# An MLP's two products by seven block products instead of eight, with squared activations kept in DRAM

## The chip, the cores and the metric

The kernel runs on one core of a Trainium2 chip. The metric is the device time of one execution in microseconds. A core has five engines that run side by side and each take their instructions in a fixed order: TensorE (PE in the profile; PEld is its loading of weights), VectorE (DVE), ScalarE (ACT), GpSimd (POOL) and SyncE (SP), which here issues the transfers between DRAM and the on-chip memory SBUF. TensorE writes its sums into eight banks of a second memory, PSUM.

## The reference, cut to what matters

A trunk of two layers over 1024 tokens of width 1024. Each layer has a token mixer, a cross-attention into 256 memory tokens and an MLP with 4096 hidden features (d_ff); each of the three starts with an RMSNorm and ends with a residual sum. All is float32.

```python
def rmsnorm(x, g):
    y = x * lax.rsqrt(jnp.mean(x * x, axis=-1, keepdims=True) + EPS)
    return y * g

def sq_relu_mlp(h, w_in, w_out):          # (1024, 1024) @ (1024, 4096), then @ (4096, 1024)
    return jnp.square(jax.nn.relu(h @ w_in)) @ w_out

for i in range(DEPTH):                    # DEPTH = 2
    ...
    h = h + sq_relu_mlp(rmsnorm(h, norm_mlp[i]), mlp_w_in[i], mlp_w_out[i])
return rmsnorm(h, norm_final)
```

## The kernel before

Everything lies feature by token: a tile is 128 features by 512 tokens, so the residual stream x is eight tiles for each of two chunks c of 512 tokens. To keep float32's precision with TensorE's faster format (fp32r), every operand is split into a high part h, rounded by ScalarE, and a low part l, the exact rest, a subtraction (`split_l`, L89) on GpSimd or VectorE. `mm3` (L101) makes a product of three matmuls: h·h, h·l, l·h. One matmul has a 128x128 block of weights and 512 columns of activations.

`load_w` (L91) loads 128x512 weights through SP's queue and splits them: ScalarE rounds (L97), GpSimd subtracts (L89).

The norm in front of a product is spread around it: `ready` (L201) takes a finished tile of x, multiplies it with the norm's gain (`gain_split`, L188 to L192) and splits it, before 1/rms is known; the sum of squares is gathered on the way (`Norm.add`, L123), and 1/rms is multiplied into the product's result.

`mlp` (L844) goes over d_ff in 8 parts of four tiles. `win(f)` (L848) makes one tile of d_ff for both chunks: 8 x 3 matmuls each, then VectorE multiplies with 1/rms (L854) and makes relu and square in one operation (L855), ScalarE rounds (L858), GpSimd subtracts (L859). For each part, `ounit` (L870) multiplies it with its rows of w_out, eight tiles of outputs for each chunk with 4 x 3 matmuls each, and VectorE adds the result to x (L233). The squared activations g never leave SBUF. An MLP has 2 x 1536 = 3072 matmuls.

Tiles come from pools with a number of slots by tag, used in turn (2 KB per partition each); a tile can be written when the last reader of its slot is done:

```python
SLOTS = dict(x=16, a=32, g=24, o=8, p=6, f=4, raw=3, w=8, pt=4, tmp=5)
PSLOTS = dict(s=3, pt=2, acc=3)
```

Which instruction follows which on an engine is set by a scheduler when the program is built, within what data and slots allow. At run time the order is fixed, and an engine that waits holds up all that stands behind it.

## Time and profile before

| | |
|---|---|
| three runs | 2743.97, 2744.0, 2748.67 us; median 2744.0 |
| span of the profiled execution | 2743.0 us |
| TensorE busy | 2662.9 us, 97% |
| VectorE, ScalarE, GpSimd busy | 1373.9, 970.3, 1029.2 us |
| a stretch in the first MLP, 640 to 1300 us | TensorE busy 660.0 of 660 us |
| a stretch in the second MLP, 2030 to 2680 us | TensorE busy 650.0 of 650 us |

An engine is busy while it works on an instruction. Matmuls are pipelined, so the busy time of one is longer than the distance between two; the distance tells how fast TensorE goes. "PEclk" is the granted share of TensorE's full clock: 1.00 is 2.4 GHz, 0.50 is 1.2 GHz.

### The profile page before, as it was taken

What the parts mean: (1) busy time and instruction counts of PE and PEld (TensorE: products, weight loads), DVE (VectorE), ACT (ScalarE), POOL (GpSimd) and SP (SyncE); (2) the same over time, 40 slices, a digit from 0 to 9 for tenths busy, and PEclk for the clock granted to TensorE, in tenths of its full rate; (3) what the DMA queues carried; (4) which work ended last, traced back from release to release, by engine and by line L of the source; (5) the groups of instructions that cost most, each with busy time, mean ns of one, the idle gap of its engine ahead of it and who ended that gap; (6) DMA issues with size and microseconds to landing.
All of it is one profiled execution on the core that took longest, in us unless ns stands there. A gap on an engine that the chain in (4) does not pass through costs nothing.

```text
span 2743.0 us, 34762 instructions
## 1 busy us (share of the span) xinstructions
PE 2662.9 (97%) x13446; PEld 2239.1 (82%) x13446; DVE 1373.9 (50%) x2504; ACT 970.3 (35%) x1956; POOL 1029.2 (38%) x788
## 2 busy tenths in 40 slices
PE   8899999999999999999999999999999999999997
PEld 6788889787888888888888888877878888888886
DVE  6777776874222222223475766687762222222227
ACT  7677676552111111112343333345531111111112
POOL 3543235544333333343423232246253333333332
PEclk9999999999999999999999999999999999999998
DMA  3000003111111111111111010122021111111111
GB/s 118 28 23 23 27 21 97 31 43 46 54 50 50 43 46 58 47 50 35 32 32 39 24 39 24 39 70 62 24 62 46 54 43 46 54 46 52 38 50 62
DMA packets 70164, 125.48 MB, mean 46 GB/s; under 512 B 7792, under 2 KB 12656, under 8 KB 70000
## 3 DMA queue, kind: packets, MB, share of 16 engines
q1 hardware_dynamic: 69856, 123.15, 15.1%
q8 instruction: 105, 1.72, 0.3%
q14 instruction: 59, 0.48, 0.1%
q10 hardware_dynamic: 144, 0.13, 0.0%
HBM read 119.05 MB, written 4.19 MB: 45 GB/s over the span
## 4 chain that ended last, share of the span: by engine, by line
PE 82%; DVE 12%; ACT 2%; issue 2%; POOL 1%; DMA 0%; SPq 0%; DVEq 0%; ACTq 0%; POOLq 0%
PE ps_acc L104 16%; PE ps_acc L103 16%; PE ps_acc L102 16%; PE ps_s L104 9%; PE ps_s L102 9%; PE ps_s L103 9%; PE ps_s L370 4%; DVE f L434 2%; PE ps_pt L392 2%; DVE a L192 2%; DVE p L439 1%; DVE x L233 1%; DVE tmp L131 1%; DVE tmp L181 1%; PE ps_s L775 1%
## 5 line engine op out<-in xcount | busy, mean ns | idle before, releaser
L89 POOL TENSOR_TENSOR w<-raw,w 128x512 fp32r<-128x512 f32 (+1 forms) x293 | 385.4, 1317 | 586.8 <-ACT w L97 567.0
L233 DVE TENSOR_TENSOR x<-ps_acc,x 128x512 f32<-128x512 f32 x408 | 278.1, 686 | 331.8 <-PE ps_acc L104 330.2
L97 ACT CAST w<-raw 128x512 fp32r<-128x512 f32 (+1 forms) x293 | 178.8, 611 | 438.4 <-PE ps_s L103 209.2
L102 PE MATMUL ps_acc<-a,w 128*128 128x512 f32 (+1 forms) x776 | 300.9, 388 | 10.1 <-DVE tmp L349 5.2
L104 PE MATMUL ps_acc<-a,w 128*128 128x512 f32 (+1 forms) x776 | 301.0, 388 | 1.0 <-POOL w L89 1.0
L103 PE MATMUL ps_acc<-a,w 128*128 128x512 f32 (+1 forms) x776 | 299.3, 386 | 1.6 <-DVE a L192 1.5
L89 POOL TENSOR_TENSOR g<-tmp,g 128x512 fp32r<-128x512 f32 x120 | 158.2, 1320 | 295.8 <-ACT g L184 237.3
L89 POOL TENSOR_TENSOR g<-pt,g 128x512 fp32r<-128x512 f32 x96 | 124.3, 1294 | 278.9 <-ACT g L858 278.9
L233 DVE TENSOR_TENSOR x<-ps_s,x 128x512 f32<-128x512 f32 x120 | 82.9, 691 | 228.1 <-PE ps_s L104 228.1
L858 ACT CAST g<-pt 128x512 fp32r<-128x512 f32 x96 | 59.5, 620 | 349.9 <-DVE pt L855 349.9
L102 PEld LDWEIGHTS ps_acc<-a,w 128*128 128x128 f32 x776 | 147.5, 190 | 39.7 <-DVE tmp L349 5.8
L854 DVE TENSOR_TENSOR pt<-ps_acc,tmp 128x512 f32<-128x512 f32 x64 | 44.1, 691 | 259.8 <-PE ps_acc L104 251.0
L103 PEld LDWEIGHTS ps_acc<-a,w 128*128 128x128 f32 x776 | 147.4, 190 | 31.9 <-DVE a L192 5.0
L104 PEld LDWEIGHTS ps_acc<-a,w 128*128 128x128 f32 x776 | 147.4, 190 | 30.1 <-POOL w L89 1.4
L89 POOL TENSOR_TENSOR p<-raw,p 128x512 fp32r<-128x512 f32 x73 | 97.2, 1331 | 175.6 <-ACT p L97 161.7
L854 DVE TENSOR_TENSOR pt<-ps_s,tmp 128x512 f32<-128x512 f32 x64 | 44.2, 691 | 236.9 <-PE ps_s L104 233.7
L104 PE MATMUL ps_s<-g,w 128*128 128x512 f32 (+1 forms) x378 | 148.2, 392 | 0.0
L102 PE MATMUL ps_s<-g,w 128*128 128x512 f32 (+1 forms) x378 | 148.0, 392 | 0.0
L103 PE MATMUL ps_s<-g,w 128*128 128x512 f32 (+1 forms) x378 | 148.0, 391 | 0.0
L102 PE MATMUL ps_acc<-g,f 128*128 128x512 f32 (+1 forms) x377 | 146.2, 388 | 0.0
L103 PE MATMUL ps_acc<-g,f 128*128 128x512 f32 (+1 forms) x377 | 146.2, 388 | 0.0
L104 PE MATMUL ps_acc<-g,f 128*128 128x512 f32 (+1 forms) x377 | 145.9, 388 | 0.0
(242 smaller groups left out, 7001.6 us busy)
## 6 DMA issues: line engine op xcount, KB each, us to landing
raw<-in_w_in SPq DMA_DIRECT2D x128, 256.0 KB, 2.6
raw<-in_w_out SPq DMA_DIRECT2D x128, 256.0 KB, 2.6
x<-in_xT SPq DMA_DIRECT2D x16, 256.0 KB, 5.1
raw<-in_w_mo SPq DMA_DIRECT2D x16, 256.0 KB, 2.7
raw<-in_w_xk SPq DMA_DIRECT2D x16, 256.0 KB, 2.7
raw<-in_w_xv SPq DMA_DIRECT2D x16, 256.0 KB, 2.7
raw<-in_w_xq SPq DMA_DIRECT2D x16, 256.0 KB, 2.6
raw<-in_w_xo SPq DMA_DIRECT2D x16, 256.0 KB, 2.6
```

What stands on the lines that cost most here:

```text
L89: eng.tensor_tensor(out=l, in0=full, in1=h.bitcast(F32), op=ALU.subtract)
L97: nc.scalar.copy(out=h, in_=raw)
L102: nc.tensor.matmul(out=ps, lhsT=wh, rhs=xh, start=start, stop=False, skip_group_check=True)
L103: nc.tensor.matmul(out=ps, lhsT=wh, rhs=xl, start=False, stop=False, skip_group_check=True)
L104: nc.tensor.matmul(out=ps, lhsT=wl, rhs=xh, start=False, stop=stop, skip_group_check=True)
L192: nc.vector.scalar_tensor_tensor(out=l, in0=xt, scalar=g, in1=h.bitcast(F32), op0=ALU.mult, op1=ALU.subtract)
L233: nc.vector.tensor_tensor(out=x[c][f], in0=ps, in1=x[c][f], op=ALU.add)
L370: nc.tensor.matmul(out=ps[:, :n], lhsT=lh, rhs=rh, start=(i == 0), stop=(i == len(passes) - 1), skip_group_check=True)
L392: nc.tensor.transpose(out=tp[:, o0:o0 + P], in_=col(probs[qi][kb // 4], kb % 4), identity=ident)
L434: nc.vector.tensor_tensor_scan(out=rev, data0=rev, data1=pt[j][:, :n], op0=ALU.mult, op1=ALU.bypass, initial=1.0 if j == len(pieces) - 1 e ...
L854: nc.vector.tensor_tensor(out=t, in0=ps, in1=r[c], op=ALU.mult)
L858: nc.scalar.copy(out=h, in_=t)
```

## The change

Both products of the MLP are cut into 2x2 blocks and made by Strassen's scheme in the form with 15 sums: seven block products instead of eight. For C = A·B with A a block of weights (transposed) and B activations, the chunks of tokens are B's two column halves. The weights' sums are S1 = A21 + A22, S2 = S1 - A11, S3 = A11 - A21, S4 = A12 - S2; those of B are T1 to T4. Products go into three banks: A11·B11 and then A12·B21 on top of it, S2·T2, S3·T3 and A22·T4 in the second, S1·T1 and S4·B22 in the third; VectorE and ScalarE read a bank between two products (`e1` to `e7`).

The first four of the 32 tiles of d_ff are left as they were (their squares go to DRAM and come back at the end); the other 28 are taken in 14 pairs. `ready` now waits for 1/rms and makes normalised tiles; `quad` makes T1 to T4 of them. `win` makes one pair: four loads of weights, `weight_sums` (four sums on VectorE, seven splits by ScalarE and GpSimd), seven products of 12 matmuls, relu and square, and the sums T1 to T4 for the second product, four operations; seven tiles are stored to DRAM. After all pairs, `fetch` loads and splits a pair's seven tiles, and `wout` adds the last up to four pairs to two tiles of outputs for both chunks; over 17 steps each of four such output pairs takes all 14.

```diff
     def ready(c, f, gcol):
+        if gcol in (G_MLP, G_MLP + 8):
+            norm[c].add(x[c][f], nc.vector if f % 2 else nc.gpsimd)
+            if f == FT - 1:
+                rms[c], norm[c] = norm[c].finish(), Norm(D)
+                for k in range(FT):
+                    t = T("p")
+                    normed(t, c, k, gcol)
+                    act[c].append(split(t, "a", nc.vector if k % 2 else nc.gpsimd))
+            return
...
+    SEVEN = (("A11", "B11", 0), ("S2", "T2", 1), ("A12", "B21", 0), ("S3", "T3", 1), ("S1", "T1", 2), ("A22", "T4", 1),
+             ("S4", "B22", 2))
...
+    def weight_sums(load, n):
+
+        w, pe, ve = n * P, nc.gpsimd, nc.vector
+        a11, a12, a21, a22 = (load(q, ("raw", "f", "raw", "f")[q]) for q in range(4))
+        s1, s2 = T("tmp")[:, :w], T("tmp")[:, :w]
+        r = {"A11": split(a11, "w", pe)}
+        tt(ve, s1, a21, a22, ALU.add)
+        tt(ve, s2, s1, a11, ALU.subtract)
+        r["S2"] = split(s2, "p", pe)
+        r["A12"] = split(a12, "w", pe)
+        tt(ve, a21, a11, a21, ALU.subtract)
+        r["S3"] = split(a21, "p", pe)
+        r["S1"] = split(s1, "w", pe)
+        r["A22"] = split(a22, "p", pe)
+        tt(ve, s2, a12, s2, ALU.subtract)
+        r["S4"] = split(s2, "w", pe)
+        return r
...
+            for t, c, f in ((b11, 0, k), (b12, 1, k), (b22, 1, k + 4), (b21, 0, k + 4)):
+                normed(t, c, f, gcol)
+            tt(nc.vector, b11, b12, b11, ALU.subtract)
+            tt(nc.gpsimd, b12, b22, b12, ALU.subtract)
+            tt(nc.vector, b22, b22, b11, ALU.subtract)
+            tt(nc.vector, b21, b21, b22, ALU.subtract)
+            for name, t, tag in (("T1", b11, "g"), ("T3", b12, "g"), ("T2", b22, "g"), ("T4", b21, "o")):
+                b[name].append(split(t, tag, nc.gpsimd if name in ("T3", "T4") else nc.vector))
...
+            wa = weight_sums(load, 4)
+            p1, u2, u3, g11 = T("pt"), T("pt"), T("pt"), T("tmp")
+
+            def square(t):
+                nc.scalar.activation(out=t, in_=t, func=AF.Relu)
+                nc.scalar.activation(out=t, in_=t, func=AF.Square)
...
+            def e3(ps):
+                nc.scalar.activation(out=g11, in_=ps, func=AF.Relu)
+                nc.vector.tensor_tensor(out=g11, in0=g11, in1=g11, op=ALU.mult)
...
+            def e7(ps):
+                tt(nc.vector, u2, ps, u2, ALU.add)
+                square(u2)
+
+            seven(wa, b, 4, ("s", "acc")[n % 2], (e1, e2, e3, e4, e5, e6, e7))
+
+            g21, g12, g22 = p1, u2, u3
+            t1, t2, t4 = (T("tmp") for _ in range(3))
+            tt(nc.gpsimd, t1, g12, g11, ALU.subtract)
+            tt(nc.vector, g12, g22, g12, ALU.subtract)
+            tt(nc.vector, t2, g22, t1, ALU.subtract)
+            tt(nc.vector, t4, g21, t2, ALU.subtract)
+            spilt[kp] = {}
+            for name, t in (("B11", g11), ("B21", g21), ("B22", g22), ("T1", t1), ("T3", g12), ("T2", t2), ("T4", t4)):
+                d = spilt[kp][name] = dram(f"{name}_{kp}")
+                nc.sync.dma_start(out=d, in_=t)
...
+            for name, tag, eng in (("B11", "a", nc.gpsimd), ("T2", "g", nc.vector), ("B21", "a", nc.gpsimd),
+                                   ("T3", "g", nc.vector), ("T1", "g", nc.vector), ("T4", "o", nc.gpsimd),
+                                   ("B22", "a", nc.vector)):
+                t = T("tmp")
+                nc.sync.dma_start(out=t, in_=spilt[kp][name])
+                r[name] = split(t, tag, eng)
...
+            def e4(ps):
+                tt(nc.vector, u3, ps, p1, ALU.add)
+                tt(nc.gpsimd, x22, x22, u3, ALU.add)
+                tt(nc.gpsimd, x21, x21, p1, ALU.add)
+                tt(nc.gpsimd, x12, x12, u2, ALU.add)
...
+        for t in range(len(pairs) + 3):
+            if t < len(pairs):
+                fetch(pairs[t])
+            mp = (t + 1) % 4
+            end = min(t + 1, len(pairs))
+            if end > done[mp]:
+                wout(t, mp, pairs[done[mp]:end])
+                done[mp] = end
```

What the scheduler makes of it is shown at two places, first in the first product. VectorE there before (pt holds a result, tmp is 1/rms):

```order
L854 TENSOR_TENSOR pt_8825<-ps_acc_8800,tmp_6811 128x512
L855 SCALAR_TENSOR_TENSOR pt_8825<-pt_8825 128x512
L854 TENSOR_TENSOR pt_8857<-ps_s_8832,tmp_7120 128x512
L855 SCALAR_TENSOR_TENSOR pt_8857<-pt_8857 128x512
L854 TENSOR_TENSOR pt_8901<-ps_s_8876,tmp_6811 128x512
```

Each result is two operations (L854, L855), and no weights pass VectorE. VectorE at the same place of the changed kernel, between two pairs of the first layer (L874 is the helper `tt`). pt_8557 is u2, pt_8558 u3, pt_8556 p1 of a pair, tmp_8661 its T1, tmp_8662 T2, tmp_8663 T4; tmp_8690 and tmp_8691 are s1 and s2 of the next pair.

```order
L874 TENSOR_TENSOR pt_8557<-ps_s_8562,pt_8557 128x512
L874 TENSOR_TENSOR pt_8557<-pt_8558,pt_8557 128x512
L874 TENSOR_TENSOR tmp_8662<-pt_8558,tmp_8661 128x512
L874 TENSOR_TENSOR tmp_8663<-pt_8556,tmp_8662 128x512
L874 TENSOR_TENSOR tmp_8690<-raw_8686,f_8688 128x512
L874 TENSOR_TENSOR tmp_8691<-tmp_8690,raw_8682 128x512
```

The sums of the next pair's weights stand behind the last sums of this one's activations. GpSimd there (L90 is `split_l`): tmp_8661 is the difference T1, then come the low parts of S1, S2, S3, A22 and S4 of the next pair and of A11 of the pair after it.

```order
L874 TENSOR_TENSOR tmp_8661<-pt_8557,tmp_8559 128x512
L90 TENSOR_TENSOR w_8712<-tmp_8690,w_8711 128x512
L90 TENSOR_TENSOR p_8699<-tmp_8691,p_8698 128x512
L90 TENSOR_TENSOR p_8708<-raw_8686,p_8707 128x512
L90 TENSOR_TENSOR p_8716<-f_8688,p_8715 128x512
L90 TENSOR_TENSOR w_8721<-tmp_8691,w_8720 128x512
L90 TENSOR_TENSOR w_8861<-raw_8850,w_8860 128x512
```

T1 stands in this row ahead of the next pair's splits. ScalarE there: relu and square of u2, the high part of S1, the relu of the next pair's first block (L966, after A11·B11 and A12·B21), the high part of S2, which is what TensorE's next matmul reads.

```order
L956 ACTIVATE pt_8557<-pt_8557 128x512
L957 ACTIVATE pt_8557<-pt_8557 128x512
L159 CAST w_8711<-tmp_8690 128x512
L966 ACTIVATE tmp_8727<-ps_acc_8728 128x512
L159 CAST p_8698<-tmp_8691 128x512
```

The copy of s2 (p_8698) stands behind the tail of the pair before. TensorE there (activations, then weights): the end of S4·B22 of a pair, then S2·T2 (ps_acc_8729) and S1·T1 (ps_acc_8730) of the next.

```order
L103 MATMUL ps_s_8562<-a_7438,w_8552 128x512
L104 MATMUL ps_s_8562<-a_7439,w_8552 128x512
L105 MATMUL ps_s_8562<-a_7438,w_8553 128x512
L103 MATMUL ps_acc_8729<-g_7534,p_8698 128x512
L104 MATMUL ps_acc_8729<-g_7535,p_8698 128x512
L103 MATMUL ps_acc_8730<-g_7526,w_8711 128x512
L104 MATMUL ps_acc_8730<-g_7527,w_8711 128x512
L105 MATMUL ps_acc_8730<-g_7526,w_8712 128x512
```

S2·T2 directly follows the last product of the pair before; A11·B11 and A12·B21 of each pair have moved ahead into the pair before it, between that pair's S2·T2 and A22·T4.

The second place is the second product, GpSimd's row. Before, where w_out and activations are split:

```order
L89 TENSOR_TENSOR g_9285<-pt_9281,g_9284 128x512
L89 TENSOR_TENSOR g_9329<-pt_9325,g_9328 128x512
L89 TENSOR_TENSOR w_9587<-raw_9584,w_9586 128x512
L89 TENSOR_TENSOR g_9361<-pt_9357,g_9360 128x512
L89 TENSOR_TENSOR o_9405<-pt_9401,o_9404 128x512
```

Its row is low parts alone. In the changed kernel, most of one step of the second product (w and p are parts of weights, a of fetched activations, x of the residual stream):

```order
L90 TENSOR_TENSOR w_11633<-raw_11614,w_11632 128x512
L874 TENSOR_TENSOR x_226<-x_226,pt_11473 128x512
L90 TENSOR_TENSOR w_11643<-f_11618,w_11642 128x512
L90 TENSOR_TENSOR p_11639<-tmp_11631,p_11638 128x512
L90 TENSOR_TENSOR w_11652<-tmp_11630,w_11651 128x512
L90 TENSOR_TENSOR a_11767<-tmp_11764,a_11766 128x512
L90 TENSOR_TENSOR p_11648<-raw_11622,p_11647 128x512
L874 TENSOR_TENSOR x_234<-x_234,pt_11474 128x512
L90 TENSOR_TENSOR a_11779<-tmp_11776,a_11778 128x512
L90 TENSOR_TENSOR w_11661<-tmp_11631,w_11660 128x512
```

Additions to x, which wait for results of TensorE, now stand between the splits.

## Rows read from the trace of the kernel before

**Rows 1.** The page: busy time and share by engine; the chain that ended last, by engine.
```profile
PE 2662.9 (97%) x13446; PEld 2239.1 (82%) x13446; DVE 1373.9 (50%) x2504; ACT 970.3 (35%) x1956; POOL 1029.2 (38%) x788
...
PE 82%; DVE 12%; ACT 2%; issue 2%; POOL 1%; DMA 0%; SPq 0%; DVEq 0%; ACTq 0%; POOLq 0%
```
**Rows 2.** Stretches: length, busy us (instructions) of PE, PEld, DVE, ACT, POOL; PEclk, DMA, GB/s.
```profile
590.00:640.00 50.00, 47.00 (x205) 37.90 (x204) 35.98 (x58) 21.59 (x37) 26.72 (x19) 0.97 0.20 59
640.00:1300.00 660.00, 660.00 (x2889) 542.25 (x2888) 177.64 (x250) 117.83 (x193) 236.13 (x185) 1.00 0.16 48
2030.00:2680.00 650.00, 650.00 (x2848) 534.15 (x2848) 174.20 (x241) 112.23 (x184) 233.23 (x182) 1.00 0.17 48
```
**Rows 3.** Timeline in the first MLP: start us, length us, engine, line, operation, [idle before, releaser].
```profile
801.38 0.40 PE L104 MATMUL ps_s<-o,w 128*128 128x512 f32 x1
...
801.61 0.40 PE L102 MATMUL ps_s<-g,w 128*128 128x512 f32 x1
...
801.81 0.69 DVE L233 TENSOR_TENSOR x<-ps_s,x 128x512 f32<-128x512 f32 x1 [2.10 <-PE ps_s L104]
...
804.42 0.62 ACT L97 CAST w<-raw 128x512 fp32r<-128x512 f32 x1 [10.43 <-PE ps_s L103]
...
805.12 1.29 POOL L89 TENSOR_TENSOR w<-raw,w 128x512 fp32r<-128x512 f32 x1 [9.75 <-ACT w L97]
```
**Rows 4.** Groups by form: count | busy us, mean ns | idle before, releasers.
```profile
L233 DVE TENSOR_TENSOR x<-ps_acc,x 128x512 f32<-128x512 f32 x408 | 278.1, 686 | 331.8 <-PE ps_acc L104 330.2
...
L97 ACT CAST w<-raw 128x512 fp32r<-128x512 f32 x273 | 169.4, 621 | 423.7 <-PE ps_s L103 209.2 <-PE ps_acc L103 137.4 <-issue 68.7
...
L89 POOL TENSOR_TENSOR g<-pt,g 128x512 fp32r<-128x512 f32 x96 | 124.3, 1294 | 278.9 <-ACT g L858 278.9
...
L89 POOL TENSOR_TENSOR w<-raw,w 128x384 fp32r<-128x384 f32 x12 | 12.4, 1036 | 33.5 <-ACT w L97 33.5
L89 POOL TENSOR_TENSOR w<-raw,w 128x256 fp32r<-128x256 f32 x8 | 6.9, 862 | 4.3 <-ACT w L97 4.2
```
**Rows 5.** Timeline of VectorE around the first MLP's start.
```profile
611.39 1.77 DVE L131 TENSOR_TENSOR tmp<-tmp 128x512 f32<-128x512 f32 x1
...
618.20 1.25 DVE L144 TENSOR_SCALAR sm_v<-sm_v 128x4 f32<-128x4 f32 x1
619.36 0.68 DVE L131 TENSOR_TENSOR tmp<-tmp 128x512 f32<-128x512 f32 x1
...
641.12 1.28 DVE L855 SCALAR_TENSOR_TENSOR pt<-pt 128x512 f32<-128x512 f32 x2
```
**Rows 6.** Timeline of GpSimd in the same stretch.
```profile
604.51 5.15 POOL L131 TENSOR_TENSOR tmp<-tmp 128x512 f32<-128x512 f32 x3
...
610.98 1.64 POOL L89 TENSOR_TENSOR w<-raw,w 128x512 fp32r<-128x512 f32 x1
...
617.78 1.64 POOL L89 TENSOR_TENSOR w<-raw,w 128x512 fp32r<-128x512 f32 x1
```
**Rows 7.** Timeline of TensorE in the second mixer, after a wait.
```profile
1398.35 0.39 PE L102 MATMUL ps_acc<-pt,g 128*128 128x256 f32 x1 [2.79 <-ACT pt L167]
...
1399.58 0.63 PE L102 MATMUL ps_acc<-a,w 128*128 128x512 f32 x1
1400.01 0.63 PE L103 MATMUL ps_acc<-a,w 128*128 128x512 f32 x1
```
**Rows 8.** Stretches of 1 us there, columns as in rows 2.
```profile
1398.00:1399.00 1.00, 0.65 (x3) 0.60 (x4) 0.67 (x2) 1.00 (x3) 1.00 (x1) 0.95 0.03 8
1399.00:1400.00 1.00, 1.00 (x3) 0.73 (x3) 0.83 (x3) 0.91 (x3) 0.18 (x1) 0.50 0.00 0
...
1402.00:1403.00 1.00, 1.00 (x5) 0.79 (x5) 0.96 (x2) 0.00 (x0) 0.00 (x0) 0.84 0.00 0
1403.00:1404.00 1.00, 1.00 (x6) 0.82 (x5) 1.00 (x2) 0.00 (x0) 0.00 (x0) 1.00 0.00 0
```
**Rows 9.** Transfers: tile, queue, count, KB each, median us from issue to landing.
```profile
raw<-in_w_in SPq DMA_DIRECT2D x128, 256.0 KB, 2.6
...
out_y<-a SPq DMA_DIRECT2D x16, 256.0 KB, 2.2
```

More of the change, by code (lines that the diff above doesn't have):

```diff
@@ L57, in trunk_kernel @@
     pp = ctx.enter_context(tc.tile_pool(name="pp", bufs=1, space=bass.MemoryType.PSUM))
+    dr = ctx.enter_context(tc.tile_pool(name="dr", bufs=1, space=bass.MemoryType.DRAM))
     def T(tag, dt=F32):
@@ L152, in finish, with split @@
             return (y, spread(y, q, self.acc)) if along else y
+    def split(src, tag, eng):
+        w = src.shape[-1]
+        h, l = T(tag, F32R)[:, :w], T(tag, F32R)[:, :w]
+        nc.scalar.copy(out=h, in_=src)
+        split_l(l, src, h, eng)
+        return h, l
     def steps(ws, per, act, ps):
@@ L199, in trunk_kernel, with normed @@
     rms = [None, None]
+    def normed(t, c, f, gcol):
+        nc.vector.scalar_tensor_tensor(out=t, in0=x[c][f], scalar=gains[:, gcol + f:gcol + f + 1], in1=rms[c][1],
+                                       op0=ALU.mult, op1=ALU.mult)
     def ready(c, f, gcol):
+        if gcol in (G_MLP, G_MLP + 8):
[7 more added lines that the diff above has]
+            return
         h, l = T("a", F32R), T("a", F32R)
@@ new lines, in trunk_kernel, with tt @@
+    SEVEN = (("A11", "B11", 0), ("S2", "T2", 1), ("A12", "B21", 0), ("S3", "T3", 1), ("S1", "T1", 2), ("A22", "T4", 1),
+             ("S4", "B22", 2))
+    def tt(eng, out, a, b, op):
+        eng.tensor_tensor(out=out, in0=a, in1=b, op=op)
+    def weight_sums(load, n):
[14 more added lines that the diff above has]
+        return r
```

152 lines of the change are left out of this document (109 added, 43 removed).

## The prediction

> **What bounds the kernel now.** I read the page first: TensorE is busy 97% of the 2743.0 us span, and 82% of the chain that ended last is TensorE [rows 1]. Then the table by stretch of time, for the two MLPs: from 640 to 1300 us and from 2030 to 2680 us TensorE has no idle time at all, while VectorE works 27% and GpSimd 36% of the stretch [rows 2]. 2889 matmuls in 660 us are 0.228 us each, and two neighbours in the timeline start 0.23 us apart [rows 2, 3]. An MLP has 3072 matmuls, 700 us; the two are half the kernel, and nothing but the number of matmuls sets their time. Whoever removes matmuls there gains 0.228 us for each, as long as the other engines deliver.
>
> **What is removed.** In each layer four of the 32 tiles of d_ff stay as they were (192 + 192 matmuls). The other 28 go as 14 pairs: 14 x 84 = 1176 matmuls per product, before 28 x 48 = 1344. So 336 fewer per layer, 672 in all: 672 x 0.228 = 153 us. If TensorE stayed full, the kernel would take 2591 us.
>
> **What the removal costs.** I price four places per layer, and sum over two layers. The durations [rows 4]: 0.69 us for a VectorE operation that reads PSUM, 0.62 for a ScalarE copy, 1.29 for a GpSimd subtraction of a 512 wide tile, 1.04 and 0.86 at widths 384 and 256. Two VectorE operations that don't wait for each other start 0.6 us apart [rows 5]. A matmul's result reaches VectorE 0.2 us after the next matmul has started, and GpSimd starts 0.08 us after ScalarE's end [rows 3]. ScalarE to VectorE or TensorE I take as 0.05.
>
> One more price comes from the timeline before the first MLP. VectorE's addition of two SBUF tiles takes 0.68 us alone, but 1.77 when a GpSimd operation is under way, and even an operation on 128x4 values takes 1.25 [rows 5]; each ends about half a microsecond after GpSimd's end, or with it. Three GpSimd operations with VectorE's between them take 5.15 us, 1.72 each instead of 1.29 [rows 6]. So the two exclude each other: a VectorE operation between two GpSimd ones costs GpSimd some 0.45 us. Those with a PSUM operand keep 0.686 in the mean of 408 [rows 4]. The changed MLP has many operations with both inputs in SBUF: all weight sums, the sums of squared activations, half the splits.
>
> The Trainium skill (SBUF — State Buffer, section "SBUF: two separate sides") calls this an exclusive lock that VectorE and GpSimd hold for a whole instruction. By that rule a pair would cost 0.69 + 1.29 = 1.98 us; the row says 1.72, so some of the operation lies outside the lock. In the second product below the rule would give 13 x 1.29 + 8 x 0.69 = 22.3 us a step and the row 20.4.
>
> *The first product, a pair of tiles.* Its 84 matmuls need 19.2 us; GpSimd has 8 operations (10.3 us), VectorE 13, ScalarE 15: as a sum everything fits beside TensorE. The order doesn't let it. VectorE's row after the last product of a pair is: final sum of that product, three sums of squared activations, and only then the two weight sums of the next pair. The row of TensorE has S2·T2 of the next pair directly behind the last product, S4·B22. So TensorE waits for this chain, counted from the end of the last matmul: VectorE's sum 0.2 + 0.69; ScalarE's relu and square, two times 0.66, to 2.2; GpSimd's difference, to 3.6; VectorE's three sums and the weight sum s1, four at 0.6 to 0.7, to 6.2; then on ScalarE the copy of s1, the relu of the next pair's A11 result, which was queued ahead, and the copy of s2, to 7.9. TensorE stands still for 8.0 us, in every pair.
>
> After it, GpSimd still owes six subtractions until A11 of the pair after is split, with two VectorE operations between: from 7.4 us, 6 x 1.29 + 2 x 0.45 = 8.6, to 16.0. TensorE needs that for its 27th matmul. The other 58 follow: 16.0 + 58 x 0.228 = 29.2. In between TensorE has 8 us for 26 matmuls. After a wait of 2.79 us the trace shows the lower of the clock's two levels (1.2 GHz, granted 0.50) for some 3.5 us, and a pitch of 0.43 [rows 7, 8]; here that is 8 slow and 18 full matmuls, 7.5 us: GpSimd's debt covers it. I take 29.5 us a pair: 14 x 29.5 = 413 us against 1344 x 0.228 = 306 before, **+107**. From below: the stall without clock loss or debt, 27.2, +75. From above: 32.5, +149, if the clock is low for twice as long or a store is late. On the store: the relu queued ahead of the copy of s2 writes a buffer whose predecessor must have been stored to DRAM; that store is issued at 3.6, and the relu comes at 6.8. Stores of 256 KB land in 2.2 us and loads in 2.6 [rows 9], so 0.6 us are spare.
>
> The Trainium skill (DMA: Bandwidth & Descriptors, "Anatomy of one DMA") puts most of a transfer's fixed time on the confirmation of the write, and HBM as the slowest target. The row for stores to DRAM contradicts it for this size, 2.2 against 2.6; if it held under this load, each further microsecond would cost 28 us in all.
>
> *Before it: normalised inputs.* Until now the first product took x times gain and was scaled behind the product; TensorE lost 3 us around the start of the MLP [rows 2]. Now every tile waits for the norm's end, and all of B's sums (`quad`, all four) must be there before the first S2·T2. From the end of cross-attention I count 68 VectorE operations with SBUF inputs (16 normed tiles and 8 splits in `ready`; 28 normed or summed and 8 splits in the quads; 8 squares) and 30 on GpSimd (8 + 4 + 8 splits and sums, 8 weight splits, 2 for the first pair): 30 pairs of 1.72 and 38 x 0.6 = 74 us, and 5 for the norm's last steps. TensorE has 192 + 24 matmuls to do meanwhile, 49 us. 79 - 49 - 3 = **+27**. From below +10 (VectorE's 68 at 0.6 alone, and 20 us of waits), from above +36.
>
> *Between the products.* The fetch of squared activations stands on SP's queue behind the stores of the last pair, which wait for its whole tail: 5.5 us, a store 2.2, a load 2.6, a copy and a subtraction 2: **+12** (8 to 16). SP's queue alone is moved past here; ScalarE and GpSimd issue no transfers.
>
> *The second product, a step of four pairs.* GpSimd has 13 operations (three splits of fetched tiles, seven of weights, three additions to x): 13 x 1.29 + 8 x 0.45 = 20.4 us against TensorE's 19.2; I take 22, since the row of GpSimd mixes operations that wait for three engines. 11 such steps are 242 us. The first three, with one to three pairs, have nearly all of GpSimd's work but few matmuls: 14 + 16 + 18 = 48. The last three, without fetches, go by TensorE, 29. 319 against 306: **+13**. From below: TensorE full and 20 us lost in the first steps, 268 + 20, -18. From above 26 a step, +61.
>
> *The last tiles of d_ff* are as before, with eight loads and splits: +2 (0 to 5). Attention and cross-attention are the same but for 16 tiles that VectorE and ScalarE no longer scale there: nothing, since TensorE is the wait there.
>
> Sum per layer: 27 + 107 + 12 + 13 + 2 = 161; for two, 322. The profiled execution's span is 2743.0 and the runs' median 2744.0, so 1 us lies around it: **2744 + 322 = 3066 us**.
>
> **Rivals.**
> 1. *Faster: the stall of the first product isn't there.* If each pair ran at TensorE's 19.2, the first product would give back 38 us a layer, and with the other places at their lower ends (10 + 8 - 18 + 0 = 0) the kernel would take 2744 - 76 = 2668. With the other places at these ends it decides at 21.9 us a pair: less than 2.7 us of idle time per pair, and the change wins. For it: the sums of each engine's work are below TensorE's. Against it: the chain is a row of dependent operations on in-order engines. 3%.
> 2. *Cheap: only the chain counts.* 27.2 a pair, second product at TensorE's pace plus its start: 2744 + 2 x (20 + 75 + 10 - 10 + 0) = 2934. For it: rows that exclude each other are few in the trace. 20%.
> 3. *Dear: GpSimd bounds the second product* at 26 us a step, with the first at 30.5: 2744 + 2 x (30 + 121 + 14 + 61 + 3) = 3202. For it: 13 operations in order, each waiting for ScalarE, a DMA or TensorE. Against: before, they ran 36% busy without trouble. 20%.
> 4. *The low clock stays* through most of a pair: 8 + 84 x 0.43 = 44 us, 3066 + 28 x 14.5 = 3472. Against: [rows 8] has the full level again after 3.5 us of work. 4%.
>
> **Chances and range.** My forecast, from 2980 to 3140, has 53%; faster 3%, cheap 20%, dear 20%, low clock 4%. The range takes in the cheap and the dear case: 2920 to 3220. A measurement of this kernel tells 0.2% (5 us) from no change; the cases that end there are slivers of the first two: faster 0.03, same 0.01, slower 0.96.
>
> **What would show it.** TensorE idle about 8 us before the first matmul that uses S2 in each of 28 pairs, released by ScalarE's copy of s2, with VectorE's row of five operations in front; the granted clock at 0.50 behind it. A second, short wait on GpSimd at A11. GpSimd over 85% busy in the second product, and TensorE waiting for its splits. Some 30 us of TensorE idle in the first 80 us of each MLP. I am wrong if the pairs come closer than 25 us, or if VectorE's and GpSimd's operations overlap at full speed.

## The result, and the profile after

The changed kernel takes **3066.7 us** (median of four runs, 3063.1 to 3068.5) against 2745.6 for the kernel before beside it: **1.117 times as long, 95% interval 1.115 to 1.118**. Its profiled execution spans 3066.7 us. Of its page, the busy times, beside [rows 1], and the granted clock in 40 slices (tenths of full speed):

```profile
PE 2653.0 (87%) x12774; PEld 2177.3 (71%) x12774; DVE 1875.7 (61%) x2960; ACT 1279.0 (42%) x2556; POOL 1519.3 (50%) x1124
...
PEclk9999999988888879999999999999988888799998
```

TensorE has 672 matmuls fewer, 5%, and yet is busy almost as long as before, 2653 us for 2663; its idle time has grown from 80 to 414 us. The 8s and 7s in the clock's row stand where the MLPs are: part of the matmuls there run at half clock and take longer. The first MLP by stages, columns as in [rows 2]: the entry, twelve pairs of the first product, and most of the second product.

```profile
616.00:691.00 75.00, 54.77 (x218) 42.32 (x217) 73.00 (x84) 27.93 (x48) 44.62 (x28) 0.86 0.15 46
...
726.00:1083.00 357.00, 262.11 (x1009) 206.59 (x1009) 129.35 (x157) 104.50 (x182) 135.72 (x97) 0.85 0.28 96
...
1158.00:1385.00 227.00, 205.26 (x855) 162.64 (x855) 148.57 (x149) 86.99 (x158) 195.03 (x135) 0.98 0.45 134
```

At the entry VectorE has no room left, 73 us of 75. In the first product nobody is full: TensorE stands still for 95 of 357 us, and no other engine is busy for more than 136. In the second product GpSimd is busy 86%.

The waits of TensorE by line and releaser (total us, times, longest us) name the first product's idle time. These two rows are waits for ScalarE's copies of weight sums, 230 us in 34 waits over both layers; 28 of them stand in front of a pair's S2·T2:

```profile
PE ps_s L103 <- ACT p L159: 116.6, 16, 9.7
PE ps_acc L103 <- ACT p L159: 113.7, 18, 7.8
```

One such wait in the timeline, all engines in order of time (columns as in [rows 3]; the last matmul before it starts at 896.89):

```profile
896.89 0.39 PE L105 MATMUL ps_s<-a,w 128*128 128x512 f32 x1
...
897.32 0.69 DVE L874 TENSOR_TENSOR pt<-ps_s,pt 128x512 f32<-128x512 f32 x1 [2.05 <-PE ps_s L105]
...
898.04 0.63 ACT L956 ACTIVATE pt<-pt 128x512 f32<-128x512 f32 x1 [1.45 <-DVE pt L874]
898.71 0.63 ACT L957 ACTIVATE pt<-pt 128x512 f32<-128x512 f32 x1
899.41 1.26 POOL L874 TENSOR_TENSOR tmp<-pt,tmp 128x512 f32<-128x512 f32 x1 [14.61 <-ACT pt L957]
...
900.71 0.69 DVE L874 TENSOR_TENSOR pt<-pt 128x512 f32<-128x512 f32 x1 [2.69 <-POOL tmp L874]
901.32 1.41 DVE L874 TENSOR_TENSOR tmp<-pt,tmp 128x512 f32<-128x512 f32 x2
...
902.64 0.69 DVE L874 TENSOR_TENSOR tmp<-raw,f 128x512 f32<-128x512 f32 x1
903.36 0.69 DVE L874 TENSOR_TENSOR tmp<-tmp,raw 128x512 f32<-128x512 f32 x1
903.42 0.62 ACT L159 CAST w<-tmp 128x512 fp32r<-128x512 f32 x1 [4.08 <-DVE tmp L874]
903.94 0.59 ACT L966 ACTIVATE tmp<-ps_acc 128x512 f32<-128x512 f32 x1
...
904.43 0.61 ACT L159 CAST p<-tmp 128x512 fp32r<-128x512 f32 x1
...
905.09 0.79 PE L103 MATMUL ps_acc<-g,p 128*128 128x512 f32 x1 [7.81 <-ACT p L159]
```

Read it downwards: the last product's sum, relu, square, GpSimd's difference, three sums of activations (900.71 to 902.7), then s1 and s2 of the *next* pair's weights, on ScalarE the copy of s1, the relu that stands ahead, and the copy of s2, at whose end TensorE starts. Each row starts within 0.1 us of the end of what it waits for: the row above it or, for the copy of s1, s1's sum. The weights that s1 and s2 are made of had been loaded long before: their four transfers were issued from 875.3 to 881.1 us, and none of the stretch takes more than 3.6 us to land.

Behind it the granted clock, in stretches of 1 us (PE alone: length, busy us, matmuls that touch the stretch, PEclk, DMA, GB/s), and two neighbours in the timeline at either level:

```profile
906.00:907.00 1.00, 1.00 (x4) 0.50 0.50 182
...
909.00:910.00 1.00, 1.00 (x4) 0.68 0.00 0
910.00:911.00 1.00, 1.00 (x6) 1.00 0.63 76
```
```profile
906.11 0.63 PE L103 MATMUL ps_acc<-g,w 128*128 128x512 f32 x1
...
906.53 0.63 PE L104 MATMUL ps_acc<-g,w 128*128 128x512 f32 x1
...
910.51 0.40 PE L105 MATMUL ps_acc<-g,p 128*128 128x512 f32 x1
...
910.74 0.40 PE L103 MATMUL ps_acc<-g,p 128*128 128x512 f32 x1
```

Matmuls start 0.42 us apart at 0.50 (the lower of the two levels, 1.2 GHz) and 0.23 us apart at 1.00.

The stages of the first layer beside the prediction's terms. For the entry both kernels are compared at equal counts of matmuls: the changed one has done 3536 when its first S2·T2 starts, and the kernel before, with 3494 at 660 us and 0.228 us each, gets there at 669.5. The products are compared with the 306 us that either takes before.

```profile
0.00:690.80 690.80, 643.62 (x3536) 0.98 0.16 47
```

| stage, us a layer | predicted | measured |
|---|---|---|
| entry | +27 | +21 (690.8 - 669.5) |
| first product | 413, +107 | 413, +107 |
| between the products | +12 | +9 (one wait of 8.83) |
| second product | 319, +13 | 331, +25 |
| last tiles | +2 | about 0 |
| sum | 161 | 162 |

The rounded terms add up to 162; counted directly, by the matmuls done at 1485 us, the first layer has lost 160. Between the medians lie 321 us, 161 a layer. That is the predicted sum to the microsecond, and the last digits are luck: of its five terms four were off by 2 to 12 us, three too high and one too low.

### The profile page after: what moved, and what is told of

Its sections match the earlier page's. It is cut to its first block, busy times and chain, and to the rows that moved or that the text cites. A ratio compares the mean times of both kernels' runs of the same rounds, so it can differ in the third digit from the quotient of the medians.

```text
span 3066.7 us, 36800 instructions
## 1 busy us (share of the span) xinstructions
PE 2653.0 (87%) x12774; PEld 2177.3 (71%) x12774; DVE 1875.7 (61%) x2960; ACT 1279.0 (42%) x2556; POOL 1519.3 (50%) x1124
## 5 line engine op out<-in xcount | busy, mean ns | idle before, releaser
L90 POOL TENSOR_TENSOR w<-raw,w 128x512 fp32r<-128x512 f32 (+3 forms) x251 | 332.7, 1328 | 413.7 <-ACT w L98 370.3
L103 PE MATMUL ps_acc<-a,w 128*128 128x512 f32 (+1 forms) x932 | 364.5, 392 | 20.1 <-ACT w L159 6.2
L105 PE MATMUL ps_acc<-a,w 128*128 128x512 f32 (+1 forms) x932 | 363.1, 390 | 2.1 <-POOL w L90 1.7
L104 PE MATMUL ps_acc<-a,w 128*128 128x512 f32 (+1 forms) x932 | 362.1, 389 | 2.2 <-DVE a L201 1.5
L90 POOL TENSOR_TENSOR g<-tmp,g 128x512 fp32r<-128x512 f32 x120 | 158.1, 1319 | 297.0 <-ACT g L193 238.6
L103 PE MATMUL ps_s<-a,w 128*128 128x512 f32 (+1 forms) x528 | 212.3, 402 | 48.1 <-ACT a L159 22.2
L874 POOL TENSOR_TENSOR tmp<-pt,tmp 128x512 f32<-128x512 f32 x28 | 35.3, 1261 | 411.9 <-ACT pt L957 411.9
L103 PEld LDWEIGHTS ps_acc<-a,w 128*128 128x128 f32 x932 | 177.9, 191 | 60.9 <-ACT w L159 8.9
L90 POOL TENSOR_TENSOR w<-tmp,w 128x512 fp32r<-128x512 f32 (+3 forms) x124 | 167.5, 1354 | 102.2 <-ACT w L159 93.9
L104 PE MATMUL ps_s<-a,w 128*128 128x512 f32 (+1 forms) x528 | 211.0, 400 | 6.7 <-POOL a L90 3.6
L105 PE MATMUL ps_s<-a,w 128*128 128x512 f32 (+1 forms) x528 | 209.1, 396 | 2.9 <-POOL w L90 2.8
L105 PEld LDWEIGHTS ps_acc<-a,w 128*128 128x128 f32 x932 | 178.3, 191 | 41.3 <-POOL w L90 6.0
L104 PEld LDWEIGHTS ps_acc<-a,w 128*128 128x128 f32 x932 | 177.9, 191 | 39.0 <-DVE a L201 5.0
L874 DVE TENSOR_TENSOR pt<-ps_acc,pt 128x512 f32<-128x512 f32 x102 | 70.2, 688 | 216.0 <-PE ps_acc L105 212.8
L103 PE MATMUL ps_s<-g,p 128*128 128x512 f32 x224 | 97.5, 435 | 120.4 <-ACT p L159 116.6
L103 PE MATMUL ps_acc<-g,p 128*128 128x512 f32 x224 | 96.6, 431 | 115.5 <-ACT p L159 113.7
L98 ACT CAST w<-raw 128x512 fp32r<-128x512 f32 (+2 forms) x189 | 114.3, 606 | 192.3 <-PE ps_acc L104 148.1
L874 DVE TENSOR_TENSOR pt<-ps_s,pt 128x512 f32<-128x512 f32 x106 | 72.8, 687 | 197.4 <-PE ps_s L105 196.5
L874 POOL TENSOR_TENSOR x<-x,pt 128x512 f32<-128x512 f32 x102 | 151.6, 1488 | 14.7 <-DVE pt L874 13.5
L103 PEld LDWEIGHTS ps_s<-a,w 128*128 128x128 f32 x528 | 102.2, 193 | 79.1 <-ACT a L159 23.5
```

Source lines behind the costliest of these rows:

```text
L90: eng.tensor_tensor(out=l, in0=full, in1=h.bitcast(F32), op=ALU.subtract)
L98: nc.scalar.copy(out=h, in_=raw)
L103: nc.tensor.matmul(out=ps, lhsT=wh, rhs=xh, start=start, stop=False, skip_group_check=True)
L104: nc.tensor.matmul(out=ps, lhsT=wh, rhs=xl, start=False, stop=False, skip_group_check=True)
L105: nc.tensor.matmul(out=ps, lhsT=wl, rhs=xh, start=False, stop=stop, skip_group_check=True)
L874: eng.tensor_tensor(out=out, in0=a, in1=b, op=op)
```

## Experiments

Ratios are to the kernel before on the same chip, four runs or more of each; a layer's times are read in the first layer. Where a run is said to take so much less than the changed kernel, the two medians come from different chips (the kernel before took 2743.4 to 2745.6 us beside them), and the runs of one kernel lie up to 12 us apart: a difference of 7 or 11 us is hardly more than that and rests on the traces.

**1. The weight sums ahead of the tail.** Theory A was the chain read above; B that VectorE and GpSimd exclude each other and their work is too much; C that the way through DRAM costs.

```diff
-        s1, s2 = T("tmp")[:, :w], T("tmp")[:, :w]
...
+        s1, s2 = T(tag)[:, :w], T(tag)[:, :w]
...
-    def seven(a, b, n, psum, evict):
+    def seven(a, b, n, psum, evict, ahead=()):
...
             ev(banks[j])
+            next(ahead, None)
```

`weight_sums` is a generator here, `ahead` that of the next pair, and `tag` is a in the first product. The edit moves the sums and gives s1 and s2 other tiles; the two were not tried apart.

> The changed kernel, but in the first product the weight sums and splits of pair n+1 are emitted one product at a time inside pair n (one after each of its seven products), and s1 and s2 lie in four tiles of the tag a that are free there. Nothing else is changed and nothing is left out. Theory A (the stall is the chain sum, relu, square, difference, three sums, s1, s2 on in-order engines): the 7.8 us of idle time before the first S2 matmul of a pair goes, with it the half clock behind it (1.6 us), and a pair takes 19.4 to 20.5 us instead of 29.4 to 30.3. 28 x 9.3 = 260 us less: 2790 to 2830 us. Rival B (VectorE and GpSimd exclude each other, so their work bounds the pair): the idle time moves to other products and the pair stays above 25 us: over 2930 us. Rival C (stores to DRAM hold the buffers): the wait turns up at the activation that needs a stored buffer: over 2900 us.

Measured 2845.2 us, 221 less than the changed kernel; ratio to before 1.036 (1.035 to 1.038). Three rows of its timeline, the first at the entry:

```profile
695.27 0.80 PE L103 MATMUL ps_s<-g,p 128*128 128x512 f32 x1 [13.74 <-ACT p L159]
...
875.60 0.50 PE L103 MATMUL ps_s<-g,p 128*128 128x512 f32 x1 [0.33 <-DVE pt L874]
...
895.59 0.50 PE L103 MATMUL ps_acc<-g,p 128*128 128x512 f32 x1 [0.33 <-DVE pt L874]
```

Pairs come every 20.0 us, some 20.9, with 0.3 to 1.2 us of waiting in place of 7.8 and the clock at 0.99 (726 to 975 us): theory A, with the gain per pair that it named. The total missed its 2790 to 2830 by 15 us. The stages around the pairs grew: the entry's last wait is 13.74 us, where the changed kernel waits 9.00, and the last pair has a wait of 5.71 us that it had not had.

**2. No stores.**

```diff
-                d = spilt[kp][name] = dram(f"{name}_{kp}")
-                nc.sync.dma_start(out=d, in_=t)
...
-                nc.sync.dma_start(out=t, in_=spilt[kp][name])
+                nc.sync.dma_start(out=t, in_=ins["w_in"][i, kp, 0])
```

> The changed kernel without the stores of the 14 pairs' squared activations to DRAM; the second product's loads read blocks of w_in instead, as many and as large, so what it multiplies is not the activations. Theory A: the pairs keep their 29.4 us, since the store of a buffer is done before the activation that needs it; only the transition shortens by the store and its wait, some 2 to 5 us a layer: 3055 to 3065 us. Rival C (the DRAM passing is what costs): the 7.8 us in front of S2 shrink by the store's 2.0 us or more, 28 x 2 = 56 us and up: under 3010 us.

This kernel leaves the stores out, so its second product multiplies other numbers. Measured 3059.4 us, 7 less. The pairs keep their wait to the hundredth, two of them here; then the first and the fourth matmul of the second product:

```profile
843.59 0.80 PE L103 MATMUL ps_acc<-g,p 128*128 128x512 f32 x1 [7.81 <-ACT p L159]
...
873.61 0.79 PE L103 MATMUL ps_s<-g,p 128*128 128x512 f32 x1 [7.81 <-ACT p L159]
...
1101.42 0.53 PE L103 MATMUL ps_s<-a,w 128*128 128x512 f32 x1 [2.62 <-ACT a L159]
...
1110.60 0.79 PE L103 MATMUL ps_s<-a,w 128*128 128x512 f32 x1 [5.90 <-ACT pt L1028]
```

The stores cost nothing in the pairs' waits, and rival C falls. Between the products the wait is 2.62 us instead of 8.83, but 5.90 us stand behind it where the changed kernel waits 1.34. At the last pair's S2·T2 this execution is 2.4 us ahead of the changed kernel's, with the same waits, and at the second product's first S2·T2 4.9: some 2.5 us lie at the transition.

**3. GpSimd's additions to x on VectorE.**

```diff
-                tt(nc.gpsimd, x22, x22, u3, ALU.add)
+                tt(nc.vector, x22, x22, u3, ALU.add)
```

(The other two additions likewise.)

> The changed kernel with the three additions to x per step of the second product on VectorE instead of GpSimd. Nothing is left out. Theory A (GpSimd, 86% busy there, bounds a step, and a VectorE operation between two of GpSimd's costs it 0.45 us): GpSimd has 10 operations instead of 13, 10 x 1.5 = 15 us, a step goes from 22.4 us towards TensorE's 19.4 and the first three steps lose 2 us each: 2 x (11 x 2 + 6) = 56 us less, 3000 to 3030 us. Rival (a step is bound by VectorE, whose late addition frees the PSUM bank for A22 T4): three more VectorE operations of 0.7 to 1.8 us make it later, 22.4 to 24 us a step: 3070 to 3110 us.

Measured 3055.9, 11 less: neither range. The same stretch as above, of this kernel:

```profile
1158.00:1385.00 227.00, 206.81 (x851) 163.76 (x850) 164.02 (x178) 82.85 (x151) 148.53 (x102) 0.96 0.44 128
```

GpSimd falls from 195 to 149 us, and TensorE does 851 matmuls instead of 855. The gain is in the first three steps (55.8 us instead of 61). With GpSimd 65% busy a step is no shorter, so in this kernel its work does not bound the steady steps. For the changed kernel the edit alone does not settle it, since it also gives VectorE three operations more. In the changed kernel's stretch VectorE waits most for GpSimd's additions to x:

```profile
DVE x L874 <- POOL x L874: 19.5, 7, 4.3
```

These waits are gone here, but in front of the same line VectorE now waits 33.7 us in nine waits for ScalarE.

**4. The entry's work on VectorE alone.**

```diff
-            norm[c].add(x[c][f], nc.vector if f % 2 else nc.gpsimd)
+            norm[c].add(x[c][f], nc.vector)
...
-                    act[c].append(split(t, "a", nc.vector if k % 2 else nc.gpsimd))
+                    act[c].append(split(t, "a", nc.vector))
```

(The quads' splits and their one difference on GpSimd likewise.)

> The changed kernel with all of GpSimd's work on inputs before the first pair moved to VectorE: half the norm's additions, half the splits of normed tiles, one difference and two splits of each quad, 28 operations a layer; GpSimd keeps the weights' splits. Nothing is left out. Theory A (the two engines exclude each other there): 20 operations of 0.6 us come to VectorE's chain and 20 pairs that took 1.1 us more than that vanish, -10 us a layer: 3040 to 3052 us. Rival (the engines work beside each other, and VectorE is only long of work, 73 us of 75): 20 x 0.62 = 12 us more a layer, 3085 to 3100 us.

Measured 3051.3, 15 less. From 616 us to the first S2·T2, to be read against the 75 us above:

```profile
616.00:680.50 64.50, 52.52 (x213) 42.30 (x213) 62.03 (x98) 27.28 (x48) 14.00 (x8) 0.89 0.16 54
```

VectorE does 98 operations in 62.0 us where 84 took 73.0, and GpSimd 8 where it had 28. More operations in less time on the engine that bounds the stage: the two exclude each other.

**5. s1 and s2 of the second product out of tmp.**

```diff
-            wa = weight_sums(load, len(win_))
+            wa = weight_sums(load, len(win_), "a")
```

> The changed kernel; only s1 and s2 of the second product's weight sums lie in tiles of the tag a that are free there, so that the five tiles of tmp serve the fetched activations alone. Nothing is left out. With the additions to x on VectorE GpSimd fell from 86% to 65% of the steady second product and a step stayed near 22 us, so GpSimd's work is not its bound. Theory D (the loads of activations and weights wait on SP's queue for the five tmp tiles, the splits stand at the head of VectorE's queue until they land, and the sums that free the PSUM banks come late): a step falls from 22.4 to 20 to 21 us, 2 x 11 x 2 = 44 us less, 3010 to 3040 us. Rival E (the weight sums and splits of a step come late by their place in the order, whatever the buffers): no change, 3055 to 3075 us.

Measured 3046.6, 20 less, between the two ranges: a step goes from 21.7 to 21.2 us in the mean of the eleven full ones (924 matmuls), and the first three gain some. Buffers are a small part of the loss.

**6. Normalised inputs alone, in the kernel before.**

```diff
-                nc.vector.tensor_tensor(out=t, in0=ps, in1=r[c], op=ALU.mult)
-                nc.vector.scalar_tensor_tensor(out=t, in0=t, scalar=0.0, in1=t, op0=ALU.max, op1=ALU.mult)
+                nc.scalar.activation(out=t, in_=ps, func=AF.Relu)
+                nc.vector.tensor_tensor(out=t, in0=t, in1=t, op=ALU.mult)
```

`ready` and `normed` are those of the changed kernel.

> The kernel before with one part of the change alone: the MLP's inputs are normalised before they are split, and the first product is not scaled behind it (relu on ScalarE, square on VectorE). Both products have all their eight blocks, there are no quads and nothing passes through DRAM; nothing is left out. In the changed kernel's trace TensorE waits some 10 us a layer for normalised tiles between 616 and 651 us, where the kernel before waits 3. Theory: this part costs 5 to 9 us a layer of the 21 that the entry costs, 2754 to 2764 us; the rest is the quads'. Rival (the wait for the norm is most of the entry's cost): 2775 us and more. Rival (it is hidden): 2740 to 2750 us.

Measured 2775.5, 32 more than before: ratio 1.012 (1.010 to 1.013), the second of the three cases, at its lower edge. The start of the MLP, this kernel and then the kernel before:

```profile
616.00:660.00 44.00, 32.24 (x121) 24.16 (x120) 34.57 (x45) 17.37 (x31) 25.54 (x17) 0.81 0.13 34
```
```profile
616.00:660.00 44.00, 41.00 (x180) 33.33 (x179) 23.46 (x47) 13.68 (x23) 22.86 (x18) 0.96 0.19 60
```

59 matmuls fewer in these 44 us (64 fewer counted from the start, 14.6 us), of which 9 us are idle time and the rest the half clock behind each wait; from 660 to 1300 us the two kernels do the same number (2803 and 2801). So normalising first, by itself, costs two thirds as much as the whole entry's 21 us. In the changed kernel it costs less: there 45 matmuls are missing at 660 us, 10.3 us, in part since TensorE waits 0.87 us for the second chunk's norm where this kernel waits 3.59. Counted from the start, the changed kernel and then the kernel before:

```profile
0.00:660.00 660.00, 623.41 (x3449) 0.98 0.15 45
```
```profile
0.00:660.00 660.00, 630.47 (x3494) 0.99 0.15 47
```

The other half of the 21 us comes with the quads and the first weights, in two waits of 1.62 and 9.00 us.

**7. The pipelined kernel.** Everything that the first six runs pointed to, in one order: loads, sums and splits of a unit, and the fetch of its activations, are emitted product by product during the unit before, over the border between the products too.

```diff
-                    t = T("p")
+                    t = held[c, k] = T("p" if k % 4 == 3 else "g")
...
+        for k, u in enumerate(units):
+            wa, nxt, ahead = nxt, {}, []
+            if k + 1 < len(units):
+                ahead.append(sums(k + 1, coming.pop(k + 1), nxt))
+                if units[k + 1][0] == "out" and units[k + 1][1] < len(pairs):
+                    ahead.append(fetch(pairs[units[k + 1][1]]))
```

`units` are the 14 pairs and the 17 steps in a row; `held` keeps the normalised tiles for the quads. Not shown: the work of experiments 3 and 4 and all splits of fetched tiles are on VectorE, as are those of the plain tiles' weights in the first product, s1 and s2 lie in a as in experiments 1 and 5, and the plain tiles' squares are on ScalarE.

> The changed kernel with its work in another order; nothing is left out. In both products weight sums and splits are emitted one product at a time during the unit before, their loads one product earlier still, and the fetch of the next pair's activations likewise, also over the border between the products; s1 and s2 lie in the tag a; the additions to x and all splits of fetched tiles are on VectorE. At the entry all work on inputs is on VectorE, the normalised tiles are kept and not made twice (32 operations a layer become 16), and the squares of the plain tiles are on ScalarE. Theory (order and buffers, not the amount of work, set the loss): entry 74 to 60 us, pairs 20 us, transition 1 to 3 us instead of 9, second product 290 to 300 instead of 331: 2845 - 2 x 65 = 2715 us, 2690 to 2750. Rival (VectorE and GpSimd exclude each other and bound both products by their amount of work): steps of the second product stay at 22 us or more and the kernel at 2780 us or more.

Measured **2728.2**, inside the range; ratio 0.994 (0.993 to 0.996), the first version that beats the kernel before. What each of its parts gives was not tried. A full step of the second product still takes 20.7 us (899 matmuls in 221 us; the 21.2 of the next expectation is too long), against 19.4 at TensorE's pace.

**8. and 9. GpSimd's work given to VectorE.** In the pipelined kernel, first in the second product, then in both:

```diff
-    def weight_sums(ld, n, r):
+    def weight_sums(ld, n, r, pe):
...
-            tt(nc.gpsimd, t1, g12, g11, ALU.subtract)
+            tt(nc.vector, t1, g12, g11, ALU.subtract)
```

`pe`, the engine of the weights' splits, is VectorE for the steps in the one kernel and for pairs and steps in the other, which alone has the second edit.

> The pipelined kernel with the splits of the weights in the second product on VectorE too: GpSimd does nothing there. Nothing is left out. Before, in the steady second product of the pipelined kernel, VectorE was busy 119 of 150 us, many of its operations on SBUF tiles took 1.78 us instead of 0.69, GpSimd was busy 76 us, and a step took 21.2 us. Theory (the two engines exclude each other on SBUF tiles): VectorE's 28 operations a step take 28 x 0.61 = 17.1 us with no pair left, the PSUM sums come in time, and a step takes 19.5 to 20.5 us: 2 x 11 x 1.2 = 26 us less, 2695 to 2712 us. Rival (a shared cause other than the pairs, such as DMA traffic, lengthens VectorE's operations): they stay long, seven more of them make VectorE the bound at 22 us a step or more, 2740 us and up.

> As the pipelined kernel with all of GpSimd's work of both Strassen products on VectorE, the differences t1 of the first product too. Nothing is left out. Theory (the two engines exclude each other): the first product's VectorE has 21 operations a pair, 13 to 14 us of 19.2, and its waits of 0.3 to 1.4 us a pair shrink a little, the second product as with its splits alone on VectorE; 2685 to 2712 us, and up to 10 us below that kernel. Rival (VectorE is then too full to free the PSUM banks in time): pairs of 21 us, 2715 to 2740 us.

Measured 2701.5, inside its range, and **2683.6**, 1 us below its range and 18 below the other kernel, where up to 10 was expected; the second has a ratio of **0.978 (0.976 to 0.979)** to the kernel before. The second product's steady part, the pipelined kernel, and then with VectorE alone; below each VectorE's splits of fetched tiles by form:

```profile
1055.00:1205.00 150.00, 142.15 (x601) 113.28 (x601) 119.09 (x142) 62.11 (x108) 75.59 (x50) 0.99 0.47 132
...
L90 DVE TENSOR_TENSOR g<-tmp,g 128x512 fp32r<-128x512 f32 x22 | 22.7, 1044 | 0.0
```
```profile
1050.00:1200.00 150.00, 150.00 (x650) 121.86 (x649) 129.61 (x211) 67.77 (x115) 0.00 (x0) 1.00 0.50 147
...
L90 DVE TENSOR_TENSOR g<-tmp,g 128x512 fp32r<-128x512 f32 x23 | 15.7, 683 | 0.0
```

VectorE does 211 operations instead of 142 in hardly more time; those shown take 0.68 us each instead of 1.04, and TensorE has no idle time left. In the pipelined kernel's stretch all of TensorE's idle time, 8 us, is waits for VectorE's sums from PSUM, none for GpSimd. With both products so, thirteen pairs' worth of matmuls of the first product (13 x 84) run without a gap as well:

```profile
674.00:926.00 252.00, 252.00 (x1092) 204.76 (x1091) 168.13 (x265) 112.17 (x190) 0.00 (x0) 1.00 0.42 140
```

**10. The old order without GpSimd**, to complete the square: the changed kernel with experiments 3 and 4, and all other splits and differences of GpSimd's in the MLP, up to its last tiles, on VectorE.

```diff
-        w, pe, ve = n * P, nc.gpsimd, nc.vector
+        w, pe, ve = n * P, nc.vector, nc.vector
...
-            tt(nc.gpsimd, t1, g12, g11, ALU.subtract)
+            tt(nc.vector, t1, g12, g11, ALU.subtract)
...
-            for name, tag, eng in (("B11", "a", nc.gpsimd), ("T2", "g", nc.vector), ("B21", "a", nc.gpsimd),
+            for name, tag, eng in (("B11", "a", nc.vector), ("T2", "g", nc.vector), ("B21", "a", nc.vector),
```

> The changed kernel in its own order, with all of GpSimd's work at the entry and in both Strassen products on VectorE. Nothing is left out. It completes a square of four: the changed order and the pipelined one, each with and without GpSimd. Theory A (the order of the work costs most, the exclusion of the two engines a smaller part): the chain in front of S2 loses only GpSimd's longer difference, 7.8 to about 7.1 us, and the debt of splits behind it is paid at 0.6 us each, so a pair takes 28 us instead of 29.7: 28 x 1.5 = 42 us; the entry gives 15, the second product 20 to 50: 2955 to 2995 us. Rival B (the exclusion is what costs, and the order only shows it): pairs of 22 us or less, under 2850 us.

Measured 2940.1, ratio 1.071 (1.069 to 1.073), 15 below the range. Of the waits in front of S2 two of a row of thirteen equal ones, and the second product's full steps:

```profile
914.94 0.80 PE L103 MATMUL ps_s<-g,p 128*128 128x512 f32 x1 [7.14 <-ACT p L159]
...
943.45 0.80 PE L103 MATMUL ps_acc<-g,p 128*128 128x512 f32 x1 [7.14 <-ACT p L159]
```
```profile
1130.00:1374.00 244.00, 243.28 (x1051) 196.84 (x1049) 209.22 (x347) 105.92 (x189) 6.59 (x5) 1.00 0.44 134
```

The wait is 7.14 us, as worked out; the pairs come every 28.2 to 29.5 us, 28.9 in the mean, where 28 was expected. The second product, in its own order and with its five tiles of tmp, now runs at TensorE's pace, 19.4 us a step; the whole of it takes 290 us instead of 331. That is where the range was too careful.

The four corners, in us:

| | GpSimd shares the work | VectorE alone |
|---|---|---|
| the change's order | 3066.7 | 2940.1 |
| pipelined | 2728.2 | 2683.6 |

With VectorE alone, the order is worth 256 us, together with the buffers of experiments 1 and 5, the kept normalised tiles and the plain tiles' squares on ScalarE; what these alone give was not tried. The left column differs by 338 us, but not by the order alone: in the pipelined kernel GpSimd has only the weights' splits and one difference left. For the same reason the rows' 127 and 45 us are not one quantity. And each holds two effects that the runs do not separate, the exclusion and GpSimd's own longer operations, 1.29 us where VectorE takes 0.69.

## Why the prediction was right, point by point

**What bounds, and what is removed: right.** With the matmuls at 0.228 us and nothing else late, 153 us are there to be had; the best version ends 61 us below the kernel before. Of the missing 92 us, 54 are idle time: TensorE is idle for 134 us of that kernel's 2681, and for 80 before.

**The first product: right in the stall and the size, half right in what fills the rest.** The chain was priced at 8.0 us and takes 7.81; 29.5 us a pair, and they come every 29.4 to 30.3, 29.73 in the mean of twelve. Beside the stall and 84 matmuls at full pace a pair takes two us more. For these the prediction named GpSimd's debt of splits and the half clock, and let the debt cover the clock. The debt is there: the split of the next A11 on GpSimd ends 15.6 us after the stall began (16.0 predicted). But TensorE loses time to it, 0.3 to 0.4 us, in only four of the twelve pairs. In the other eight the half clock has outlasted the debt: it was taken as 3.5 us, from [rows 7, 8], and lasts 3.1 to 6.1 us here (7 to 15 matmuls), which costs 1.4 to 3.0 us a pair, 2.2 in the mean. That the two are nearly equal is luck, and the clock's spread makes the pairs differ. Experiment 10 bears it out: there the splits of the debt are on VectorE, the chain is 0.67 us shorter, and a pair is only 0.8 us shorter. Experiment 1 takes the chain away and with it the stall. The store's 0.6 us of slack held: experiment 2.

**The exclusion of VectorE and GpSimd: right, and worth more than it was charged.** The prediction used it as 0.45 us on GpSimd for each pair of operations. Experiments 4, 8 and 9 show that VectorE's side weighs more: its operations on SBUF tiles go from 0.69 to as much as 1.86 us, and on VectorE stand the sums that free the PSUM banks. The Trainium skill (SBUF — State Buffer, section "SBUF: two separate sides") has this as an exclusive lock that either engine holds for the whole instruction. The runs agree that it is exclusive: with GpSimd gone, VectorE's 211 operations took 130 us, where 142 had taken 119. By that rule a pair would take 1.98 us; [rows 6] have 1.72, so the measured pair stands.

**The entry: the size was near, the place of the wait half right.** Of its sum "79 - 49 - 3" the mis-sized term is the first: from 616 us to the first S2·T2 are 74.8 us, with which the sum gives 23, and 21 are measured. VectorE is busy 73 of 75 us, as the sum wanted. But it does not come as one wait at the end. TensorE also stands in four earlier waits of 1.2 to 2.1 us for normalised tiles and the norm's last steps, with the half clock behind them; half of the 21 us is lost by 660 us (experiment 6). The final wait is 9.00 us. "Some 30 us of idle time" was announced; 20 are there.

**Between the products: 9 instead of 12.** Some 2.5 us of it are the stores' (experiment 2).

**The second product: the sum was near, the mechanism wrong.** 319 was put down, 331 measured. The eleven full steps take 239 us (242 predicted) and the last three 31 (29); the first three take 61 where 48 were charged, the term that was mis-sized:

```profile
1110.00:1170.00 60.00, 41.71 (x122) 0.76 0.57 174
1170.00:1412.00 242.00, 224.31 (x936) 0.97 0.40 119
```

(PE alone, as above; the first three steps have 126 matmuls, the next eleven 924.) The prediction said that GpSimd bounds a step with 13 operations, and that TensorE would wait for its splits. GpSimd is busy 86%, as announced, but with ten operations a step is no shorter (experiment 3). In the changed kernel's stretch from 1158 to 1385 us no wait of TensorE is for GpSimd; the long ones are for VectorE's sums from PSUM (total, times, longest):

```profile
PE ps_s L103 <- DVE pt L874: 10.7, 4, 3.2
```

What holds TensorE up is VectorE's row, and what delays that row is work shared with GpSimd: without GpSimd the same order runs at 19.4 us a step (experiment 10). VectorE is not full there (149 of 227 us); it has operations of up to 1.86 us, and it waits, most of all for GpSimd's additions to x. How much each of the two adds was not separated. An agreement of 22 with 21.7 us was no proof of the cause.

**The rivals.** *Cheap* (27.2 us a pair) and *low clock stays* did not come about. *Dear* went wrong in the same way as the forecast, by GpSimd's count. *Faster* named its condition rightly, less than 2.7 us of idle time per pair and the other places at their lower ends: with 0.8 us per pair alone (experiment 1) the kernel is still slower than before, with the other places mended too (experiment 7) it is faster. The store's rule (the Trainium skill, DMA: Bandwidth & Descriptors, section "Anatomy of one DMA") was set aside for the row. That section describes transfers that GpSimd issues, and here SyncE issues them; under the changed kernel's load the rows for these still do not bear it out, stores of 256 KB landing sooner than loads:

```profile
tmp<-T SPq DMA_DIRECT2D x112, 256.0 KB, 2.9
T<-tmp SPq DMA_DIRECT2D x84, 256.0 KB, 2.1
```

## What to carry to other kernels

An algorithm that saves TensorE 5% of its matmuls adds work between two units of it; emit what the next unit needs before the tail of this one, or an in-order engine will put the two in series. Add up the operations with two SBUF inputs on VectorE *and* GpSimd as one list: handing part of it to GpSimd slowed the whole here, so try the version with VectorE alone before balancing. And an engine that is busy 86% beside the stall is a suspect, not the cause: take a quarter of its work away and look whether the stall moves, and whose waits take its place.

## What was not expected of the hardware

After equal waits of 7.81 us the lower clock level lasted 3.14 us in the pair that starts at 875.73, 4.43 in the one at 905.09, 5.71 at 934.65 and 6.14 at 845.42; what decides it is not settled by these runs. And two engines together did less per microsecond than one: at the entry 112 operations of VectorE and GpSimd took 75 us, and 106 took 64.5 when GpSimd had 20 fewer and VectorE 14 more.
